# Pairing the modulation products of the closing gates, and scaling block 0's rows at the turn between two layers

## The chip, the core and the metric

The kernel runs on one NeuronCore of a Trainium2 chip. TensorE (PE in the profile) multiplies matrices, VectorE (DVE) and ScalarE (ACT) work element by element, GpSimd (POOL) takes a few small steps, and SyncE (SP) issues the transfers from and to the chip's large memory. Each engine works through its own queue in order; semaphores tie the queues together. The metric is the time of one execution on the device in microseconds (us), the median of several runs; lower is better.

## What is computed

The kernel is one step of a two-layer trunk over 128 context tokens and 256 latent tokens of width 1024. In each layer a vector per request (`c_ctx` for the context, `c` for the latent tokens) is turned into six modulation vectors, and two residual blocks use them:

```python
def trunk_layer(x, cvec, lp, init, latent):
    mod = jax.nn.silu(cvec.astype(jnp.float32)) @ lp['w_mod'] + lp['b_mod']
    sh1, sc1, g1, sh2, sc2, g2 = jnp.split(mod[:, None, :], 6, axis=-1)
    h = rmsnorm(x, lp['norm_mix_pre']) * (1.0 + sc1) + sh1
    mix, states = mixer(h, lp, init, latent)
    x1 = x + g1 * rmsnorm(mix, lp['norm_mix_post'])
    h = rmsnorm(x1, lp['norm_ffn_pre']) * (1.0 + sc2) + sh2
    out = x1 + g2 * rmsnorm(conv_ffn(h, lp), lp['norm_ffn_post'])
    return out.astype(x.dtype), states

def conv_ffn(h, lp):
    up = jnp.einsum('bld,df->blf', h, lp['w_up'])
    a, b = jnp.split(up, 2, axis=-1)
    a = dwconv3(a, lp['ffn_conv_w'], lp['ffn_conv_b'])
    return jnp.einsum('blf,fd->bld', jax.nn.gelu(a, approximate=True) * b, lp['w_down'])
```

The change touches the products that make `g2` (the closing gate of a layer) and the step from the `out` of layer 0 to the `h` of layer 1.

## The kernel before

**Tiling.** The 384 tokens are three blocks of 128, t = 0 (context), 1 and 2 (latent). All large products are made three times with operands split into a high and a low part (`hi`, `lo` of a weight; `hh`, `hl` and `gh`, `gl` of the activations): high by high, high by low, low by high. Each weight tile arrives by a transfer (`raw`); ACT rounds it to `hi` (a CAST, L281), and DVE makes `lo` = raw - hi (L258).

**The feed-forward part** (`ffn`) runs over 32 column pairs p. `up(p)` makes the two halves a and b of pair p: 24 matmuls into PSUM bank 6 and 24 into bank 7, for every p the same two banks. `gated(p)` follows: the convolution `cv` (one ACT instruction and four DVE SCALAR_TENSOR_TENSOR, all of which read bank 6), a GELU on ACT, the product `ge` with bank 7 on DVE, the cast `gh` on ACT and the rest `gl` on DVE. `down(c)` takes the pairs 2c and 2c+1 to the three blocks in 36 matmuls into banks 0 to 5. The loop over c = 0 to 13 does `up(2c+2)`, `up(2c+3)`, `down(c)`.

**The modulation vectors.** Those that are needed later are made beside this loop, by DVE: a queue of generators (`mod_beside`) holds set 3 of the running layer (the closing gate `g2`) and, in layer 0, sets 0 to 2 of layer 1. `beside()` and `fill()` (four in each turn of the loop, after `up(2c+2)`, after `up(2c+3)`, after the first and after the second block of `down(c)`) each let the generator run to its next `yield`. For step i a transfer of one megabyte brings weight rows (`mraw`, two buffers); for each of the two vectors r DVE multiplies four strips of 512 columns by a column of `sil` and adds them to the sum `macc` (L269; the first strip of a sum is written by a TENSOR_SCALAR, L263). Set 3 has four steps i, sets 0 and 1 eight. There is a `yield` after each r, so one call makes four products. After the last one `pe_next` makes `beside()` do nothing until a `fill()`.

**The order.** A scheduler places the instructions on the queues; `issue_after` ties the products of a call behind the DVE instruction written before them, and `high_priority` draws others ahead.

**The turn to layer 1.** After `down(14)` and `down(15)` of a block, `residual` adds it to `x`, and `norm_pre` makes the sum of squares (two ACT Squares), the factor r (POOL), and here a diagonal matrix `diag` of r (DVE, 128x128). Later `norm_P` multiplies the eight pieces of the block's `x` by `diag` on PE, which scales and transposes at once. PE does this for block 0 between `down` of block 1 and of block 2. In the kernel's opening (`start`) the other form is used: `rows=True` scales the rows (`xs`, ACT), and `norm_P` then transposes them.

Of the kernel before, what the change touches and what calls it, by code (L numbers as in the profile page):

```python
# [10 lines left out]
F32 = mybir.dt.float32  # L11
F32R = mybir.dt.float32r
BF16 = mybir.dt.bfloat16
AF = mybir.ActivationFunctionType
ALU = mybir.AluOpType
# [177 lines left out]
class Trunk:  # L193
# [15 lines left out]
    def mm(self, out, lhsT, rhs, start=True, stop=True, **kw):  # L209
        with self.in_order("pe"):  # L210
            self.pe = self.nc.tensor.matmul(out, lhsT=lhsT, rhs=rhs, start=start, stop=stop, **kw)  # L211
# [207 lines left out]
    def start(self, fp):  # L419
# [67 lines left out]
        times(2)  # L487
        times(3)
        for t in range(NT):
            self.norm_pre(t, rows=True)  # L490
        self.use(md=(5,), sm=(6, 7, 0), mm=(0, 1, 2))
        taps = self.filter_taps(fp, 1, hid[1], w3[1])
        times(4)
# [130 lines left out]
    def mod_beside(self, l, s):  # L624

        nc = self.nc
        acc = [self.act_p.tile([128, 2048], F32, tag=t, name=self.nm("macc")) for t in ("hh", "hl")]
        n = KD if s < 2 else KD // 2
        for i in range(n):
            blocks = self.mod_rows(l, s, i)  # L630
            for r in range(2):
                with self.tc.issue_after(self.dve.ins):
                    for k, _, j, raw in blocks:
                        q = slice(512 * j, 512 * j + 512)
                        c = self.sil[:, k, r:r + 1]
                        if k == 0:
                            self.ts(acc[r][:, q], raw, c, ALU.mult)
                        else:
                            self.stt(acc[r][:, q], raw, c, acc[r][:, q], ALU.mult, ALU.add)
                self.pe_next = i == n - 1 and r == 1  # L640
                yield False
        self.pe_next = False
        ps = self.bank(6)

        self.narrow([
            (ps[32 * j:32 * j + 32, :], self.onesel[:, r, :], acc[r][:, 512 * j:512 * j + 512], r == 1, r == 0)
            for r in (1, 0) for j in (3, 0, 1, 2)] if s < 2 else [
            (ps[64 * r + 32 * j:64 * r + 32 * j + 32, :], self.onesel[:, r, :], acc[r][:, 512 * j:512 * j + 512], True, True)
            for r in (1, 0) for j in (1, 0)])
        self.mod_finish(l, s, ps, lambda: self.bank(7), odd=s > 1)  # L650
# [135 lines left out]
        t = lambda n: pool.tile([128, KD, T], F32R, tag=n, name=self.nm(n))  # L786
        return t("hh"), t("hl")

    def norm_pre(self, t, rows=False):

        s2 = self.tiny.tile([128, 2], F32, tag="s2", name=self.nm("s2"), bufs=6)
        for c in range(2):
            jk = self.tmp.tile([128, 512], BF16, tag="junkn", name=self.nm("junk"), bufs=1)
            self.act(jk, self.x[t][:, 512 * c:512 * c + 512], AF.Square, scale=D ** -0.5, accum_out=s2[:, c:c + 1])
        r = self.rms(s2)
        self.scaled[t] = rows
        if rows:
            self.xn[t] = [self.tmp.tile([128, 512], F32, tag="xs", name=self.nm("xs"), bufs=6) for _ in range(2)]
            for c, o in enumerate(self.xn[t]):
                self.act(o, self.x[t][:, 512 * c:512 * c + 512], AF.Copy, scale=r)  # L800
            return
        d = self.tmp.tile([128, 128], F32, tag="diag", name=self.nm("diag"), bufs=3)
        self.ts(d, self.ident, r, ALU.mult)
        self.xn[t] = d
# [659 lines left out]
    def ffn(self, l):  # L1464
        nc = self.nc
        with self.tc.tile_pool(name=f"ffn{l}", bufs=2, reuse_waits="tile") as fp:
# [63 lines left out]
            def down(c, ts=range(NT)):  # L1530
                if c not in ws:
                    ws[c] = self.weights("d", l, c)
                for t in ts:
                    tok = slice(128 * t, 128 * t + 128)
                    blocks = [(gs[p][0][:, tok], gs[p][1][:, tok], w) for p, w in zip((2 * c, 2 * c + 1), ws[c])]
                    self.token_major(accs[t], blocks, c == 0, c == 15)
# [20 lines left out]
            for t in range(NT):  # L1557
                if t == 2 and l + 1 < DEPTH:
                    self.norm_T_after(0, (l + 1, 0, 1, 0, 0), self.h1, lambda c: self.bank(6 + c))
                down(14, [t])  # L1560
                down(15, [t])
                with self.tc.high_priority(offset=300):
                    queues = [nc.sync, nc.scalar, nc.sync] if (l, t) == (DEPTH - 1, NT - 1) else [nc.sync] * 2
                    pieces = ((0, 512), (512, 1024)) if len(queues) == 2 else ((0, 512), (512, 768), (768, 1024))
                    self.residual(t, accs[t], g, pieces, lambda cols: self.store_x(l, t, cols, queues.pop(0)))
                    if l + 1 < DEPTH:
                        self.norm_pre(t)

    def store_x(self, l, t, cols, queue):
        if l + 1 < DEPTH:  # L1570
# [83 lines left out]
```

## Time and profile before

| | us |
|---|---|
| median of 3 runs | 1328.77 (1326.57 to 1328.78) |
| the profiled execution | 1326.61, its span 1324.8 |
| PE busy | 1311.8 |
| DVE busy | 911.2 |
| ACT busy | 571.8 |

The profile is of one execution. Busy times are those of each engine; a matmul on PE is shown longer than the distance to the next one, since they are pipelined, so the distance of two starts is what one costs. Times in rows count from the start of the span.

### The profile page before, as it was taken

The numbers are of one execution on the slowest core, as the hardware profiler recorded it, in microseconds if no ns is written. First come the engines' busy times: TensorE is split into PE (matmuls) and PEld (weight loads), VectorE is DVE, ScalarE is ACT, GpSimd is POOL, SyncE is SP. The second block draws the span as 40 slices with busy tenths as digits, with TensorE's granted clock in tenths as the row PEclk, the third lists the DMA queues.
The fourth block names the chain that finished last, engine by engine and source line by source line (L and its number), as shares of the span: only waits on it lengthen the run. The fifth ranks groups of instructions, "written<-read, shape, count | busy, mean of one in ns | idle before, by whom it ended". The sixth has DMA issues, their size and how long they took to land.

```text
span 1324.8 us, 19348 instructions
## 1 busy us (share of the span) xinstructions
PE 1311.8 (99%) x7465; PEld 1195.3 (90%) x7465; DVE 911.2 (69%) x1635; ACT 571.8 (43%) x950; POOL 34.0 (3%) x64
## 2 busy tenths in 40 slices
PE   8999999999999999999999999999999999999998
PEld 2689999899989989988999999988999999999997
DVE  5748776578879989888476678657885445445445
ACT  4644353473333333333367544446433333333333
POOL 1100000010000000000000000001000000000000
PEclk9999999999999999999999999999999999999999
DMA  9885442625566666665535322442454333333331
GB/s 354 306 311 171 168 137 92 221 79 172 197 218 209 218 208 212 214 215 177 173 122 180 97 84 88 133 148 113 163 182 160 127 126 129 128 127 128 127 124 52
DMA packets 61581, 218.32 MB, mean 165 GB/s; under 512 B 7262, under 2 KB 9760, under 8 KB 58160
## 3 DMA queue, kind: packets, MB, share of 16 engines
q1 hardware_dynamic: 61344, 216.94, 48.0%
q8 instruction: 59, 0.97, 0.3%
q14 instruction: 34, 0.28, 0.1%
q10 hardware_dynamic: 144, 0.13, 0.0%
HBM read 211.11 MB, written 5.94 MB: 164 GB/s over the span
## 4 chain that ended last, share of the span: by engine, by line
PE 93%; DMA 3%; DVE 2%; ACT 1%; issue 1%; POOL 0%; SPq 0%; POOLq 0%; DVEq 0%; ACTq 0%
PE b L211 91%; PE b L215 2%; DMA mraw<-in_w_mod 1%; DMA w<-in_f_w 1%; DMA lo<-in_w_mod 1%; DVE lo L258 1%; DVE x L269 0%; DVE macc L269 0%; POOL rr L294 0%; ACT hi L281 0%; SPq L545 0%; ACT junk L277 0%; DVE macc L263 0%; ACT hf L277 0%; DVE yg L258 0%
## 5 line engine op out<-in xcount | busy, mean ns | idle before, releaser
L258 DVE TENSOR_TENSOR lo<-raw,hi 128x1024 fp32r<-128x1024 f32 (+3 forms) x288 | 320.8, 1128 | 187.0 <-ACT hi L281 184.0
L281 ACT CAST hi<-raw 128x1024 fp32r<-128x1024 f32 (+3 forms) x288 | 275.4, 975 | 385.0 <-PE b L211 376.3
L211 PE MATMUL b<-hh,lo 128*128 128x384 f32 (+1 forms) x1120 | 366.8, 335 | 0.0
L211 PE MATMUL b<-hh,hi 128*128 128x384 f32 (+2 forms) x1120 | 364.0, 334 | 0.0
L211 PE MATMUL b<-hl,hi 128*128 128x384 f32 x1088 | 361.3, 337 | 0.0
L211 PEld LDWEIGHTS b<-hh,hi 128*128 128x128 f32 x1120 | 205.8, 188 | 3.0 <-ACT th L277 0.8
L211 PEld LDWEIGHTS b<-hh,lo 128*128 128x128 f32 x1120 | 208.4, 188 | 0.0
L211 PEld LDWEIGHTS b<-hl,hi 128*128 128x128 f32 x1088 | 203.7, 188 | 1.3
L269 DVE SCALAR_TENSOR_TENSOR cv<-b,pcol,cv 128x127 f32<-128x127 f32 (+1 forms) x256 | 100.5, 414 | 83.3 <-ACT cv L277 79.0
L211 PE MATMUL b<-hi,hh 128*128 128x384 f32 (+2 forms) x444 | 156.1, 355 | 0.0
L211 PE MATMUL b<-lo,hh 128*128 128x384 f32 (+2 forms) x450 | 154.1, 348 | 0.0
L211 PE MATMUL b<-hi,hl 128*128 128x384 f32 (+2 forms) x444 | 153.7, 349 | 0.0
L211 PE MATMUL b<-lo,gh 128*128 128x512 f32 x384 | 151.0, 393 | 0.5 <-DVE lo L258 0.5
L211 PE MATMUL b<-hi,gl 128*128 128x512 f32 x384 | 150.8, 393 | 0.0
L211 PE MATMUL b<-hi,gh 128*128 128x512 f32 x384 | 150.4, 392 | 0.0
L269 DVE SCALAR_TENSOR_TENSOR macc<-mraw,sil,macc 128x512 f32<-128x512 f32 x196 | 132.3, 744 | 0.0
L277 ACT ACTIVATE cv<-b,pcol 128x384 f32<-128x384 f32 x64 | 43.0, 672 | 172.4 <-PE b L211 172.1
L211 PEld LDWEIGHTS b<-hi,gh 128*128 128x128 f32 x384 | 72.1, 188 | 18.7 <-issue 4.2
L211 PEld LDWEIGHTS b<-hi,hl 128*128 128x128 f32 x444 | 83.4, 188 | 5.5 <-issue 1.9
L211 PEld LDWEIGHTS b<-hi,hh 128*128 128x128 f32 x444 | 83.4, 188 | 5.3 <-issue 1.3
L211 PEld LDWEIGHTS b<-lo,hh 128*128 128x128 f32 x450 | 84.6, 188 | 3.3 <-issue 0.5
L211 PEld LDWEIGHTS b<-lo,gh 128*128 128x128 f32 x384 | 72.1, 188 | 15.5 <-DVE lo L258 0.9
(253 smaller groups left out, 1240.4 us busy)
## 6 DMA issues: line engine op xcount, KB each, us to landing
raw<-in_w_up SPq DMA_DIRECT2D x128, 512.0 KB, 4.6
mraw<-in_w_mod SPq DMA_DIRECT2D x40, 1024.0 KB, 8.5
raw<-in_w_down SPq DMA_DIRECT2D x64, 512.0 KB, 4.1
raw<-in_w_in_r SPq DMA_DIRECT2D x32, 384.0 KB, 3.5
raw<-in_w_in_m SPq DMA_DIRECT2D x24, 384.0 KB, 4.6
raw<-in_w_out SPq DMA_DIRECT2D x16, 512.0 KB, 4.5
raw<-in_w_in_h SPq DMA_DIRECT2D x12, 512.0 KB, 4.8
mraw<-in_w_mod SPq DMA_DIRECT2D x8, 512.0 KB, 6.8
```

Of the source, the lines that this page charges most:

```text
L211: self.pe = self.nc.tensor.matmul(out, lhsT=lhsT, rhs=rhs, start=start, stop=stop, **kw)
L215: self.pe = self.nc.tensor.transpose(out, in_, self.ident[:n, :n])
L258: self.dve = self.nc.vector.tensor_tensor(o, a, b, op)
L269: self.dve = self.nc.vector.scalar_tensor_tensor(o, a, s, b, op0, op1)
L277: self.scalar = self.nc.scalar.activation(o, a, f, **kw)
L281: self.scalar = self.nc.scalar.copy(o, a)
```

## The change

It does two things.

First, in `mod_beside` the `yield` after r = 0 is left out for set 3. One call then makes the products of both vectors of a step, eight instead of four, and set 3 takes four calls instead of eight; the sets after it come four calls earlier.

Second, at the turn to layer 1 `norm_pre` of block 0 is called with `rows="both"`: DVE scales columns 0 to 511 of the rows and ACT columns 512 to 1023 (`xs`), no `diag` is made, and `norm_P` transposes `xs` with the identity. Blocks 1 and 2 stay as they were, and so does the opening.

```diff
@@ mod_beside
                 self.pe_next = i == n - 1 and r == 1
-                yield False
+                if r or s < 3:
+                    yield False
         self.pe_next = False
@@ norm_pre
-    def norm_pre(self, t, rows=False):
+    def norm_pre(self, t, rows=None):
...
         if rows:
-            self.xn[t] = [self.tmp.tile([128, 512], F32, tag="xs", name=self.nm("xs"), bufs=6) for _ in range(2)]
+            self.xn[t] = [self.tmp.tile([128, 512], F32, tag="xs", name=self.nm("xs"), bufs=6 if rows == "scalar" else 2) for _ in range(2)]
             for c, o in enumerate(self.xn[t]):
-                self.act(o, self.x[t][:, 512 * c:512 * c + 512], AF.Copy, scale=r)
+                cols = self.x[t][:, 512 * c:512 * c + 512]
+                if rows == "scalar" or c:
+                    self.act(o, cols, AF.Copy, scale=r)
+                else:
+                    self.ts(o, cols, r, ALU.mult)
             return
@@ ffn
                     if l + 1 < DEPTH:
-                        self.norm_pre(t)
+                        self.norm_pre(t, rows="both" if t == 0 else None)
```

The queue of DVE in the first turns of the loop of layer 0, from the `gl` of pair 3 to the convolution of pair 4 (`b_686` is bank 6 of pair 4). Before:

```order
L258 TENSOR_TENSOR lo_3297<-raw_3292,hi_3296 128x1024
L258 TENSOR_TENSOR gl_3283<-ge_3279,gh_3282 128x384
L263 TENSOR_SCALAR macc_3204<-mraw_3205,sil 128x512 x2
L269 SCALAR_TENSOR_TENSOR macc_3204<-mraw_3205,sil,macc_3204 128x512 x2
L269 SCALAR_TENSOR_TENSOR macc_3203<-mraw_3314,sil,macc_3203 128x512 x4
L269 SCALAR_TENSOR_TENSOR macc_3204<-mraw_3314,sil,macc_3204 128x512 x4
L258 TENSOR_TENSOR lo_3355<-raw_3350,hi_3354 128x1024
L258 TENSOR_TENSOR lo_3357<-raw_3352,hi_3356 128x1024
L269 SCALAR_TENSOR_TENSOR cv_3410<-b_686_3348,pcol_166,cv_3410 128x127 x2
L269 SCALAR_TENSOR_TENSOR cv_3410<-b_686_3348,pcol_166,cv_3410 128x255 x2
```

The same stretch with the change (bank 6 of pair 4 is `b_688` here, the weights of pair 5 are `lo_3375` and `lo_3377`, those of `down(1)` are `lo_3450` and `lo_3452`):

```order
L269 SCALAR_TENSOR_TENSOR macc_3203<-mraw_3290,sil,macc_3203 128x512 x4
L269 SCALAR_TENSOR_TENSOR macc_3204<-mraw_3290,sil,macc_3204 128x512 x4
L269 SCALAR_TENSOR_TENSOR macc_3203<-mraw_3324,sil,macc_3203 128x512 x4
L269 SCALAR_TENSOR_TENSOR macc_3204<-mraw_3324,sil,macc_3204 128x512 x4
L269 SCALAR_TENSOR_TENSOR macc_3203<-mraw_3346,sil,macc_3203 128x512 x4
L269 SCALAR_TENSOR_TENSOR macc_3204<-mraw_3346,sil,macc_3204 128x512 x4
L258 TENSOR_TENSOR lo_3375<-raw_3370,hi_3374 128x1024
L258 TENSOR_TENSOR lo_3377<-raw_3372,hi_3376 128x1024
L269 SCALAR_TENSOR_TENSOR cv_3430<-b_688_3368,pcol_166,cv_3430 128x127
L258 TENSOR_TENSOR lo_3450<-raw_3445,hi_3449 128x1024
L269 SCALAR_TENSOR_TENSOR cv_3430<-b_688_3368,pcol_166,cv_3430 128x127
L269 SCALAR_TENSOR_TENSOR cv_3430<-b_688_3368,pcol_166,cv_3430 128x255
```

Twelve products stood between that `gl` and the weights of pair 5; now 24 stand there (the products of step 0 for the second vector have gone ahead, to the call before), and two `lo` of the next weight have moved in between the four instructions of the convolution. The same difference stands in layer 1.

The queue of PE between pair 4 and pair 5. Before, the last matmuls of pair 4 (`b_687`, bank 7) are followed by those of pair 5 (`b_699`, bank 6):

```order
L211 MATMUL b_687_3349<-hl_2598,hi_3296 128x384
L211 MATMUL b_687_3349<-hh_2597,lo_3297 128x384
L211 MATMUL b_699_3429<-hh_2597,hi_3354 128x384
L211 MATMUL b_699_3429<-hl_2598,hi_3354 128x384
L211 MATMUL b_699_3429<-hh_2597,lo_3355 128x384
```

With the change, after the last matmul of pair 4 (pair 5 is `b_700`):

```order
L211 MATMUL b_646_3122<-hi_3449,gh_3199 128x512
L211 MATMUL b_647_3123<-hi_3449,gh_3199 128x512
L211 MATMUL b_648_3124<-hi_3449,gh_3199 128x512
L211 MATMUL b_649_3125<-hi_3449,gh_3199 128x512
L211 MATMUL b_650_3126<-hi_3449,gh_3199 128x512
L211 MATMUL b_651_3127<-hi_3449,gh_3199 128x512
L211 MATMUL b_646_3122<-lo_3450,gh_3199 128x512
L211 MATMUL b_646_3122<-hi_3449,gl_3200 128x512
L211 MATMUL b_646_3122<-hi_3451,gh_3286 128x512
L211 MATMUL b_647_3123<-lo_3450,gh_3199 128x512
L211 MATMUL b_646_3122<-lo_3452,gh_3286 128x512
L211 MATMUL b_700_3443<-hh_2597,hi_3374 128x384
```

Eleven of the 36 matmuls of `down(1)` have moved ahead of `up(5)`; the other 25 stay behind it.

The queue of ACT at the turn (`x_2611` is block 0, `b_648` and `b_649` the sums of block 1). Before:

```order
L277 ACTIVATE junk_6446,s_1161_6445<-x_2611 128x512
L277 ACTIVATE junk_6448,s_1161_6445<-x_2611 128x512
L277 ACTIVATE junk_6482,s_1167_6480<-b_648_3124 128x512
L277 ACTIVATE junk_6485,s_1167_6480<-b_649_3125 128x512
L277 ACTIVATE hf_6512<-b_1179_6507,modT_4647 128x128 x4
L277 ACTIVATE junk_6497,s_1173_6496<-x_2613 128x512
```

With the change:

```order
L277 ACTIVATE junk_6446,s_1161_6445<-x_2611 128x512
L277 ACTIVATE junk_6448,s_1161_6445<-x_2611 128x512
L277 ACTIVATE xs_6455<-x_2611,rr_6452 128x512
L277 ACTIVATE junk_6484,s_1168_6482<-b_648_3124 128x512
L277 ACTIVATE junk_6487,s_1168_6482<-b_649_3125 128x512
L277 ACTIVATE hf_6514<-b_1180_6509,modT_4449 128x128 x4
```

The scaling of block 0 (`xs`) has come ahead of the two Squares of block 1. On PE nothing else moved there.

## Rows read from the trace of the kernel before

**Rows 1.** The page, parts 1 and 4: busy time; the chain that ended last.

```profile
PE 1311.8 (99%) x7465; PEld 1195.3 (90%) x7465; DVE 911.2 (69%) x1635; ACT 571.8 (43%) x950; POOL 34.0 (3%) x64
...
PE 93%; DMA 3%; DVE 2%; ACT 1%; issue 1%; POOL 0%; SPq 0%; POOLq 0%; DVEq 0%; ACTq 0%
```

**Rows 2.** Timeline of DVE, layer 0: start, us, engine, line, operation, [idle before].

```profile
310.58 1.41 DVE L269 SCALAR_TENSOR_TENSOR macc<-mraw,sil,macc 128x512 f32<-128x512 f32 x2
312.22 1.64 DVE L269 SCALAR_TENSOR_TENSOR cv<-b,pcol,cv 128x127 f32<-128x127 f32 x4 [0.22 <-ACT cv L277]
...
317.79 0.55 DVE L258 TENSOR_TENSOR gl<-ge,gh 128x384 fp32r<-128x384 f32 x1
318.26 0.87 DVE L263 TENSOR_SCALAR macc<-mraw,sil 128x512 f32<-128x512 f32 x2
319.06 6.71 DVE L269 SCALAR_TENSOR_TENSOR macc<-mraw,sil,macc 128x512 f32<-128x512 f32 x10
325.69 2.35 DVE L258 TENSOR_TENSOR lo<-raw,hi 128x1024 fp32r<-128x1024 f32 x2
328.94 1.64 DVE L269 SCALAR_TENSOR_TENSOR cv<-b,pcol,cv 128x127 f32<-128x127 f32 x4 [0.91 <-ACT cv L277]
```

**Rows 3.** Timeline of ACT in the same stretch.

```profile
315.57 1.05 ACT L281 CAST hi<-raw 128x1024 fp32r<-128x1024 f32 x1 [0.64 <-PE b L211]
...
323.31 2.00 ACT L281 CAST hi<-raw 128x1024 fp32r<-128x1024 f32 x2 [6.28 <-PE b L211]
328.24 0.67 ACT L277 ACTIVATE cv<-b,pcol 128x384 f32<-128x384 f32 x1 [2.93 <-PE b L211]
```

**Rows 4.** Timeline of PE: first matmul of pair 4, first of pair 5.

```profile
323.80 0.34 PE L211 MATMUL b<-hh,hi 128*128 128x384 f32 x1
...
332.28 0.34 PE L211 MATMUL b<-hh,hi 128*128 128x384 f32 x1
```

**Rows 5.** Timeline of SyncE's issues in the same stretch.

```profile
320.49 5.68 SPq L587 DMA_DIRECT2D mraw<-in_w_mod  x2
```

**Rows 6.** Windows: stretch, us, busy per engine, PEclk, DMA share, GB/s.

```profile
324.00:325.00 1.00, 1.00 (x7) 1.00 (x6) 1.00 (x2) 1.00 (x2) 0.00 (x0) 1.00 0.85 348
325.00:326.00 1.00, 1.00 (x8) 1.00 (x7) 1.00 (x3) 0.30 (x1) 0.00 (x0) 1.00 0.24 98
```

**Rows 7.** The page, part 6: transfers, KB each, median us to landing.

```profile
mraw<-in_w_mod SPq DMA_DIRECT2D x40, 1024.0 KB, 8.5
```

**Rows 8.** Timeline of DVE, the same place in layer 1.

```profile
955.00 6.71 DVE L269 SCALAR_TENSOR_TENSOR macc<-mraw,sil,macc 128x512 f32<-128x512 f32 x10
```

**Rows 9.** Timeline of PE in the kernel's opening.

```profile
8.26 1.41 PE L211 MATMUL b<-fh,w 128*128 128x384 f32 x2 [2.05 <-DMA w<-in_f_w]
```

**Rows 10.** Windows in the opening; the third column from the right is PEclk.

```profile
6.00:9.00 3.00, 0.95 (x3) 0.30 (x2) 1.31 (x3) 0.52 (x1) 0.00 (x0) 0.91 0.97 359
9.00:12.00 3.00, 3.00 (x11) 0.30 (x9) 1.60 (x3) 0.56 (x2) 0.00 (x0) 0.52 1.00 377
```

**Rows 11.** Timeline of DVE at the turn: diagonals of blocks 0 and 1.

```profile
684.77 0.28 DVE L263 TENSOR_SCALAR diag<-c_ident,rr 128x128 f32<-128x128 f32 x1 [0.73 <-POOL rr L294]
...
690.85 0.29 DVE L263 TENSOR_SCALAR diag<-c_ident,rr 128x128 f32<-128x128 f32 x1 [0.41 <-POOL rr L294]
```

**Rows 12.** Timeline of PE at the turn: block 0, first `down` of block 2, block 1.

```profile
685.27 1.95 PE L211 MATMUL b<-diag,x 128*128 128x128 f32 x16
686.97 0.48 PE L211 MATMUL b<-hi,gh 128*128 128x512 f32 x1
...
692.56 1.95 PE L211 MATMUL b<-diag,x 128*128 128x128 f32 x16
```

**Rows 13.** The tile `xs` in the opening: duration in ns, min/median/max.

```profile
L277 ACT ACTIVATE xs<-x,rr x6: 708/720/727, 30.5 to 34.3; 128x512 f32<-128x512 f32 x6
```

**Rows 14.** The chain that ended last, in the opening: eight transposes.

```profile
43.62 1.09 PE b L215 x8
```

More of the change, by code (lines that the diff above doesn't have):

```diff
@@ L489, in start @@
         for t in range(NT):
-            self.norm_pre(t, rows=True)
+            self.norm_pre(t, rows="scalar")
         self.use(md=(5,), sm=(6, 7, 0), mm=(0, 1, 2))
```

## The prediction

> **What bounds the kernel now.** I read the page first: PE is busy 1311.8 of 1324.8 us and 93% of the chain that ended last lies on it, DVE is busy 911.2 us [rows 1]. So a change elsewhere is worth what it takes off PE's queue, or what it makes PE wait. The 69% of DVE is an average. I then read DVE's timeline at the two places that the change touches, in the first turns of the feed-forward loop of each layer and at the turn to layer 1, and beside it ACT, PE and SyncE. In the first place there is to be seen that DVE works almost without a break from 310.58 to the convolution of pair 4 at 328.94 [rows 2]: two stretches of products, with the convolution of pair 3 and the weights between them. PE starts pair 4 at 323.80 and pair 5 at 332.28, with nothing between [rows 4]. Both pairs use bank 6, so pair 5 may start only when the four DVE instructions of pair 4's convolution have read it. They end at 328.94 + 1.64 = 330.58 [rows 2], 1.7 us before PE wants the bank. That is all the room DVE has there.
>
> **Part 1, the paired products: what moves.** No product is added or removed. But the queue of DVE, in the order shown with the change, has 24 products in a row between the `gl` of pair 3 and the weights of pair 5, where 12 stood, and four products of step 0 now stand ahead of pair 3's convolution. DVE takes its queue in order, so behind them wait the `lo` of pair 5, pair 4's convolution and the `lo` of `down(1)`, and behind the convolution waits PE. I follow the queue in the times of the profile.
>
> Step 0, first vector, ends as before at 310.58 + 1.41 = 312.0 [rows 2]. The second vector's four follow: the two TENSOR_SCALAR take 319.06 - 318.26 = 0.80, the others (325.69 - 319.06)/10 = 0.66 each [rows 2], together 2.1, to 314.1. Pair 3's convolution, which started at 312.22, starts there. Its instructions take 1.64 and the two `lo` now among them some 1.15 each, half of 2.35 [rows 2]. The second `lo` needs a cast that ACT ends at 315.57 + 1.05 = 316.6, when a weight buffer comes free [rows 3], so it runs to 317.8; `ge`, ACT's cast and `gl` take about 0.55 each (the `gl` row, rows 2) and end near 319.5. Before, `gl` ended at 318.34. PE does `down(0)` meanwhile, which does not use pair 3: no cost so far, the cover is the 36 matmuls up to 323.80 [rows 4].
>
> Then 24 products at 0.66: 15.9 us, if nothing waits. The weight rows of the last step take the buffer of step 1, so SyncE can issue that megabyte only when eight of the 24 are done, at 324.8. A megabyte that had the queues nearly to itself was issued at 320.49 [rows 5], ran at 348 GB/s in 324 to 325, and by 325 to 326 the rate had fallen to 98 [rows 6]: landed after some 5.6 us. So the last eight can begin at 330.4 instead of 330.1, and end near 335.9. The median of such transfers, most with others beside them, is 8.5 us [rows 7], which would add 2.9; I take 5.6 because the two weight transfers ahead of it have their buffers by 317.8 and nothing else is issued then.
>
> After the burst come the two `lo` of pair 5, 2.35, to 338.2 (their casts on ACT end at 325.3, rows 3), then the convolution of pair 4 with the two `lo` of `down(1)` in it: 1.64 + 2.3, to about 342.1. Before, it ended at 330.58.
>
> PE ends pair 4 at 332.28 as before. The eleven matmuls of `down(1)` that now stand there are worth 11 x 0.23 = 2.5 us (24 of this form from 686.97 to 692.56, rows 12). The first six can run at once, the others need the `lo` made at about 339.7 and 341.5; all fit ahead of 342.1. Since they only come earlier than they did, pair 5 would have started at 332.28 + 2.5 = 334.8 without a wait, and starts at 342.1. **PE loses 7.3 us.** Behind it nothing is late: the `lo` of pair 5 are done at 338.2, bank 7 is free by 343, the products of the next set start only after the small matmuls that close set 3, and everything after that is the old order, one turn of the loop earlier.
>
> Layer 1 has the same queue and the same durations (955.00 and 6.71 for ten products, rows 8), and its order is changed alike: another 7.3 us. Bounds for each layer: 6.5 if the megabyte is in time and the small steps are a little shorter, 10.2 with the 8.5 us landing. A gain is excluded here: PE has no idle time at this place to give back [rows 4].
>
> **The clock after the wait.** PE does nothing from about 333.7 to 339.7 in each layer. In the opening PE waited 2.05 us up to 8.26 [rows 9], and the granted clock was 0.91 over 6 to 9 and 0.52 over 9 to 12 [rows 10]: half of full speed, 1.2 GHz, for 0.54 + 2.88 = 3.4 us in all, though PE had work again. If each of the two waits brings as long a stretch at half, each costs half of it, 1.7 us. Bounds are nothing and, with a second such stretch, 3.4 us. I take 1.7, since these idle times are longer than that in the opening. The Trainium skill says the same of TensorE (TensorE: Matmul & The Clock Gate, Part 1): the clock falls to half after an idle stretch, and sustained activity releases it. By that rule the wait costs more than its own length, and this speaks against the change; without the rule and the row the sum would be 3.4 us less.
>
> **Part 2, the turn.** Before, DVE made the diagonal of block 0 in 684.77 to 685.05 [rows 11], just in time for PE at 685.27, and the 16 records of the product held PE for 686.97 - 685.27 = 1.70 us [rows 12]. Now DVE scales 512 columns in one TENSOR_SCALAR; none of that size from `x` is shown, so I take that of the products, 0.44 to 0.48 each (0.87 for two, rows 2), ending near 685.25. ACT scales the other half in 0.72 [rows 13], from about 684.8 to 685.5, while PE transposes the first. Eight transposes took 1.09 us in the opening with their tail [rows 14], a distance of 0.11, so PE is through near 686.2: 0.8 us gained. Against this stands ACT's queue: its 0.72 comes ahead of block 1's Squares, so block 1's diagonal, ready at 690.85 + 0.29 = 691.1 [rows 11], comes near 691.8, and PE now wants it at 692.56 - 0.8 = 691.8 [rows 12]. The slack is just used up. Later the chain of DVE and ACT, not PE, sets when block 1's columns are ready. I take a gain of 0.5 us, between a gain of 0.8 and a loss of 0.7 (ACT's step paid in full, nothing gained).
>
> **Sum.** 2 x (7.3 + 1.7) - 0.5 = +17.5 us. Made against the profiled execution's 1326.61 this is 1344.1. The median of the runs, 1328.77, lies 2.2 above that execution, so I put the median after half of that higher, at 1345.
>
> **Rivals.**
> - *The wait without the clock.* PE's clock stays up, for the six matmuls and the five others inside the wait speak for activity; against it stands the opening. 1326.61 + 14.6 - 0.5 = 1340.7.
> - *The late megabyte.* The last step's rows land after 8.5 us in both layers: 1326.61 + 2 x (10.2 + 1.7) - 0.5 = 1349.9. For it speaks the median, against it that nothing else is issued.
> - *Not slower: the burst is covered.* If DVE ended pair 4's convolution by 334.8, the eleven matmuls would hide all of it and only the turn would be left, 1326.1. For this the 24 products must take 8.6 us instead of 15.9, at 0.36 each. At the TENSOR_SCALAR's distance of 0.40 they would come near; but ten and ten of the right form show 0.66 in both layers [rows 2, 8].
> - That the change does not do what it says is excluded by the order: the products do stand in a row, and the transposes are there.
>
> **How the numbers follow.** Forecast, wait and clock: 0.62. Wait without the clock 0.18, late megabyte 0.11, covered burst 0.07; 0.02 is left for faster, by nothing that I see in the rows. The range reaches from the lowest waits without the clock, 1326.61 + 13.0 - 0.8 = 1338.8, to the late megabyte on the higher median, 1328.77 + 23.3 = 1352.1: 1338 to 1352. What can be told from no change in this kernel is about 0.2%, 2.7 us. Slower by more has the first three cases, 0.91; within it the covered burst, 0.07; faster 0.02.
>
> **What would show it.** In the changed profile DVE should show 24 products in one row of some 16 us near 319.5 and again some 645 us later, pair 5's first matmul near 342 instead of 332.28, PE idle for 6 us or so before it, and a granted clock below 1 just after. At the turn PE should show eight transposes in about 1 us. The forecast is wrong if pair 5 starts by 335, if the products go faster in a row than one by one, if the clock holds, or if the wait is longer than 10 us because the last megabyte is late.

## The result

The changed kernel took 1343.96 us (median of four, 1342.85 to 1347.24) where the kernel before took 1328.25 in the same series: a ratio of 1.0128, with a 95% interval of 1.0116 to 1.0141. The profile is of the execution of 1347.24 us, whose span is 1345.5.

In the page's first part, PE, DVE and ACT:

```profile
PE 1320.2 (98%) x7457; PEld 1200.1 (89%) x7457; DVE 911.0 (68%) x1635; ACT 572.3 (43%) x951; POOL 33.7 (3%) x64
```

Beside [rows 1] the span has grown by 20.7 us. DVE does what it did, 911 us. PE is busy 8.4 us longer, though eight transposes have taken the place of sixteen records, and idle 25.3 us instead of 13.0 (span less busy). What it waited for stands in the list of PE's waits (who waits <- for whom: us in total, times, longest), of the kernel before:

```profile
PE b L211 <- DVE lo L258: 0.5, 1, 0.5
```

and of the changed kernel:

```profile
PE b L211 <- DVE lo L258: 12.5, 5, 5.3
```

So 12.0 of the 12.3 us of new idle time end at a `lo` that DVE made late: two waits of 5.3 us, one in each layer, and three short ones, two of which stand at the turn.

**Pair 5, layer 0.** DVE's timeline, to be read beside [rows 2]; this execution is 0.69 us later there than the one before, from the opening on:

```profile
313.40 1.41 DVE L269 SCALAR_TENSOR_TENSOR macc<-mraw,sil,macc 128x512 f32<-128x512 f32 x2
...
319.62 0.56 DVE L258 TENSOR_TENSOR gl<-ge,gh 128x384 fp32r<-128x384 f32 x1 [0.58 <-ACT gh L1529]
320.10 16.00 DVE L269 SCALAR_TENSOR_TENSOR macc<-mraw,sil,macc 128x512 f32<-128x512 f32 x24
336.02 2.36 DVE L258 TENSOR_TENSOR lo<-raw,hi 128x1024 fp32r<-128x1024 f32 x2
...
341.46 0.48 DVE L269 SCALAR_TENSOR_TENSOR cv<-b,pcol,cv 128x255 f32<-128x255 f32 x1
```

The 24 products are one row of 16.00 us without a break, 0.67 each, so the last megabyte came in time. The convolution of pair 4 reads bank 6 until 341.94. PE in the same stretch, beside [rows 4]:

```profile
332.97 1.54 PE L211 MATMUL b<-hi,gh 128*128 128x512 f32 x6
339.82 0.80 PE L211 MATMUL b<-lo,gh 128*128 128x512 f32 x1 [5.30 <-DVE lo L258]
...
341.26 1.13 PE L211 MATMUL b<-lo,gh 128*128 128x512 f32 x2
342.20 0.52 PE L211 MATMUL b<-hh,hi 128*128 128x384 f32 x1
```

Pair 5 starts at 342.20, a quarter of a microsecond after bank 6 is free; [rows 4] have 332.28. Without the 0.69 of the opening and the 2.5 us of matmuls that were moved ahead of it, PE has lost 6.7 us. The row at 339.82 names a `lo` of `down(1)` as what ended the idle time. That matmul is one of the eleven that were drawn ahead; pair 5 itself had to wait for bank 6, whose last reader stood behind the same row of products. The last 0.2 us are not DVE's: the eleventh matmul starts at 341.69, and at the half clock of this stretch (below) these stand 0.43 us apart, so PE is through with it at about 342.1, just after the bank is free.

Windows of the same stretch (busy per engine; the third column from the right is the granted clock):

```profile
333.00:336.00 3.00, 1.52 (x7) 0.91 (x5) 3.00 (x5) 1.05 (x1) 0.00 (x0) 1.00 0.18 68
336.00:339.00 3.00, 0.00 (x0) 0.00 (x0) 3.00 (x5) 0.00 (x0) 0.00 (x0) 0.67 0.59 177
339.00:342.00 3.00, 2.18 (x5) 1.46 (x6) 2.94 (x5) 0.00 (x0) 0.00 (x0) 0.50 0.92 321
342.00:345.00 3.00, 3.00 (x13) 3.00 (x13) 1.11 (x2) 1.03 (x2) 0.00 (x0) 0.69 1.02 404
```

The clock fell to its lower level (1.2 GHz) inside the wait and came back 1.7 us into pair 5: 2.0 + 3.0 + 1.9 = 6.8 us at half, by the three windows' clocks, most of it while PE waited or worked on the few matmuls that were moved ahead. The first 48 matmuls of pair 5 took 9.09 us instead of 8.48. In layer 1 pair 5 starts 17.68 us after pair 4 (17.71 in layer 0, 8.48 before) and takes 9.54.

**The turn.** PE, beside [rows 12]:

```profile
692.81 1.09 PE L215 MATMUL b<-c_ident,xs 128*128 128x128 f32 x8
693.66 0.48 PE L211 MATMUL b<-hi,gh 128*128 128x512 f32 x1
...
704.35 0.89 PE L211 MATMUL b<-lo,hh 128*128 128x400 f32 x4
705.71 0.45 PE L211 MATMUL b<-lo,hh 128*128 128x400 f32 x1 [0.48 <-DVE lo L258]
706.92 0.45 PE L211 MATMUL b<-lo,hh 128*128 128x400 f32 x1 [0.76 <-DVE lo L258]
707.21 0.88 PE L211 MATMUL b<-aside,hh 128*128 128x400 f32 x4
```

The transposes hold PE for 0.85 us where the diagonal's product held it for 1.70. But eleven microseconds later, in layer 1's first group, the six products with `lo` (the low parts of that group's weights) take 2.86 us; the kernel before has them in one row of 1.09, from 697.60 to 698.69:

```profile
697.60 1.25 PE L211 MATMUL b<-lo,hh 128*128 128x400 f32 x6
```

DVE at that place, with the change:

```profile
700.63 0.69 DVE L258 TENSOR_TENSOR yg<-b,G 128x512 f32<-128x512 f32 x1
...
702.11 1.42 DVE L269 SCALAR_TENSOR_TENSOR x<-yg,rr,x 128x512 f32<-128x512 f32 x2
703.44 1.05 DVE L258 TENSOR_TENSOR lo<-raw,hi 128x400 fp32r<-128x400 f32 x2
...
705.09 0.57 DVE L258 TENSOR_TENSOR lo<-raw,hi 128x400 fp32r<-128x400 f32 x1
...
706.30 0.57 DVE L258 TENSOR_TENSOR lo<-raw,hi 128x400 fp32r<-128x400 f32 x1
```

and before:

```profile
692.62 0.57 DVE L258 TENSOR_TENSOR lo<-raw,hi 128x400 fp32r<-128x400 f32 x1
693.11 0.68 DVE L258 TENSOR_TENSOR yg<-b,G 128x512 f32<-128x512 f32 x1
693.71 0.56 DVE L258 TENSOR_TENSOR lo<-raw,hi 128x400 fp32r<-128x400 f32 x1
...
696.40 1.05 DVE L258 TENSOR_TENSOR lo<-raw,hi 128x400 fp32r<-128x400 f32 x2
```

The scheduler has put these four `lo` behind the residual of block 2 (`yg`, `x`), where one of them stood ahead of it before, one in it, and the last two, at 696.40, right behind it. The last `lo` now stands behind block 2's `diag` too, for which DVE was idle 0.44 us. This execution is 7.5 us later at the turn; the last `lo` ends 9.4 us later, at 706.87, and PE comes for the six products 0.8 us earlier. So the turn lost 0.8 us instead of gaining.

### The profile page after: what moved, and what is told of

Its sections match the earlier page's. It is cut to its first block, busy times and chain, and to the rows that moved or that the text cites. A ratio compares the mean times of both kernels' runs of the same rounds, so it can differ in the third digit from the quotient of the medians.

```text
span 1345.5 us, 19326 instructions
## 1 busy us (share of the span) xinstructions
PE 1320.2 (98%) x7457; PEld 1200.1 (89%) x7457; DVE 911.0 (68%) x1635; ACT 572.3 (43%) x951; POOL 33.7 (3%) x64
```

## The experiments

Three stretches of PE's timeline are set side by side for each kernel: from the first matmul of pair 4 to the first of pair 8 in layer 0 and in layer 1, and at the turn from the first product that transposes block 0 to layer 1's first product of 384 columns with a high weight (`b<-hi,hh`). They don't depend on what an execution did elsewhere; within a loop's stretch the two spacings of the last section can make some 0.3 us of difference. Times in us; the ratio is to runs of the kernel before on the same chip.

| kernel | median | before | ratio (95%) | layer 0 | layer 1 | turn |
|---|---|---|---|---|---|---|
| before (first profile) | 1328.77 | | | 51.62 | 51.63 | 24.28 |
| changed | 1343.96 | 1328.25 | 1.0128 (1.0116 to 1.0141) | 58.74 | 59.37 | 25.09 |
| changed, again | 1348.13 | 1327.26 | 1.0145 (1.0114 to 1.0176) | 58.90 | 58.92 | 25.11 |
| part 1 alone | 1344.64 | 1328.02 | 1.0124 (1.0098 to 1.0149) | 58.62 | 58.97 | 24.27 |
| part 2 alone | 1328.52 | 1328.02 | 1.0004 (0.9994 to 1.0013) | 51.62 | 51.63 | 25.08 |
| pairs spread | 1327.56 | 1328.02 | 1.0000 (0.9990 to 1.0011) | 51.63 | 51.63 | 24.30 |
| part 2, `lo` first | 1326.72 | 1328.02 | 0.9991 (0.9982 to 1.0001) | 51.63 | 51.63 | 23.33 |
| the same, again | 1326.64 | 1327.21 | 0.9995 (0.9986 to 1.0004) | 51.63 | 51.63 | 23.36 |
| row of 20 | 1335.96 | 1327.26 | 1.0064 (1.0041 to 1.0088) | 54.50 | 55.94 | 24.27 |
| layer 1 only | 1334.89 | 1327.26 | 1.0053 (1.0033 to 1.0072) | 51.63 | 59.73 | 24.31 |
| wait filled | 1341.56 | 1327.26 | 1.0103 (1.0079 to 1.0128) | 57.17 | 57.09 | 24.25 |

**Part 1 alone.** The edit in `mod_beside` without that in `ffn`:

```diff
-                yield False
+                if r or s < 3:
+                    yield False
```

> Part 1 alone; the turn stays as in the kernel before. Theory A (from the changed kernel's trace): all of the loss is the wait of PE ahead of pair 5, 7.1 us net in layer 0 and 7.6 in layer 1, and the turn lost 0.9. Then this kernel takes 1328.3 + 14.7 = 1343.0 us, about 1 us less than the changed kernel where runs of the same matmul spacing are compared; pair 5 starts about 9.2 us later than before (6.7 of wait behind 2.5 of moved matmuls) in both layers; the stretch from the diagonals of block 0 to the first key matmuls of layer 1 takes the same 24.3 us as before. Theory B (the prediction's own terms): 9.0 per layer, and the turn gained 0.5, so 1328.3 + 18.0 = 1346.3 us, above the changed kernel.

Measured: the loop loses 7.00 us in layer 0 and 7.34 in layer 1, the turn is as before. The ratio, 1.0124, can't be told from the changed kernel's, so the whole of what can be measured in the result is part 1. The median lies between A's 1343.0 and B's 1346.3 and does not decide. The two layers' stretches agree with theory A; B's 9.0 for each layer is excluded by them.

**Part 2 alone.**

```diff
-                        self.norm_pre(t)
+                        self.norm_pre(t, rows="both" if t == 0 else None)
```

> Part 2 alone; the products come as in the kernel before. Theory A: the transposes give PE back 0.85 us, but the lo of the next weights stand behind block 2's yg and x on DVE, and PE loses 1.7 us waiting for them; net +0.85 us, 1329.1 us, with PE idle in two pieces (about 0.5 and 0.8 us, ended by lo) some 11 to 14 us after the transposes. Theory B (the prediction): no such wait, net -0.5 us, 1327.8 us. The two differ by 0.1%, so it is the rows that decide: the stretch from the first transpose to the first key matmuls (hi by hh, 128x384) of layer 1 takes 24.3 us before; A expects 25.1, B 23.8. In neither does pair 5 wait.

Measured: the loop is as before in both layers, and the turn takes 25.08 us, 0.80 more. PE shows the two waits again:

```profile
699.46 0.45 PE L211 MATMUL b<-lo,hh 128*128 128x400 f32 x1 [0.46 <-DVE lo L258]
700.67 0.45 PE L211 MATMUL b<-lo,hh 128*128 128x400 f32 x1 [0.76 <-DVE lo L258]
```

The whole kernel can't be told from the one before; the stretch can, and A's 25.1 stands against B's 23.8.

**Part 2 with the `lo` first.** In `ffn`, ahead of block 2's residual, the next weights are split, and the residual is tied behind their last `lo`:

```diff
+                early = nullcontext()
+                if l + 1 < DEPTH and t == 2:
+                    self.prep()
+                    early = self.tc.issue_after(self.dve.ins)
-                with self.tc.high_priority(offset=300):
+                with early, self.tc.high_priority(offset=300):
```

> Part 2 alone, and the weights of the next group are split ahead of block 2's residual on DVE: their lo stand before its yg and x. Theory A: the wait of PE for lo is gone and the gain of the transposes stays, -0.85 us against the kernel before, unless the yg of block 2, 1.1 to 2.2 us later, makes block 2's diagonal late (PE wants it 0.9 us earlier than before; it was ready 2.6 us ahead): 1327.5 to 1328.3 us, and the stretch from the first transpose to the first key matmuls of layer 1 takes 23.4 us. Theory B: the lo never mattered, and this equals the kernel with part 2 alone.

Measured: 23.33 us, 0.95 less than before and 1.75 less than part 2 alone. DVE has the `lo` in one row ahead of `yg`:

```profile
693.11 2.03 DVE L258 TENSOR_TENSOR lo<-raw,hi 128x400 fp32r<-128x400 f32 x4
695.05 0.69 DVE L258 TENSOR_TENSOR yg<-b,G 128x512 f32<-128x512 f32 x1
```

and PE has its six products in one row, and block 2's diagonal in time:

```profile
696.84 1.25 PE L211 MATMUL b<-lo,hh 128*128 128x400 f32 x6
...
700.84 1.95 PE L211 MATMUL b<-diag,x 128*128 128x128 f32 x16
```

So the order of those four instructions, and nothing in the scaling or the transposes, made part 2 a loss. Since this version had the lowest median of all, it ran once more.

> Part 2 with the lo of the next weights ahead of block 2's residual, once more and in more rounds, to see whether it beats the kernel before. Theory A (the stretch of the turn is 0.95 us shorter, 23.33 instead of 24.28, and nothing else differs): the ratio to the kernel before is 0.9993, 1327.3 us beside 1328.2, near the limit of what can be told. Rival: the first series' 0.9991 was chance, and the ratio is 1.000.

The ratio is 0.9995, and its interval holds 1.0000 as well as the expected 0.9993. That the turn is shorter is shown, 23.36 us; that the kernel is faster than the one before is not.

**The pairs spread out.** The products of the closing gate stay paired, but after each pair the generator yields once more, so that every other call makes none:

```diff
+                if s == 3 and r and i < n - 1:
+                    yield False
```

> Part 1 with one edit: after each pair of a step the generator of set 3 yields once more, so that a call that makes eight products is followed by one that makes none. The products are paired, their number is the same, but only eight, not 24, stand between the gl of pair 3 and the weights of pair 5; the turn stays as before. Theory A (the row of 24 in front of the convolution of pair 4 is what costs): no wait at pair 5 in either layer, half clock nowhere in the loop, 1328.3 us within 1.5. Rival C (the pairing itself costs, by the eight products in one piece ahead of a convolution or by the buffers of the weight rows): waits of some us remain, 1332 us or more.

Measured: no loss anywhere. DVE in layer 0, the stretch of [rows 2]:

```profile
318.93 0.75 DVE L269 SCALAR_TENSOR_TENSOR macc<-mraw,sil,macc 128x512 f32<-128x512 f32 x1
319.60 0.56 DVE L258 TENSOR_TENSOR gl<-ge,gh 128x384 fp32r<-128x384 f32 x1
320.07 4.72 DVE L269 SCALAR_TENSOR_TENSOR macc<-mraw,sil,macc 128x512 f32<-128x512 f32 x7
325.07 2.36 DVE L258 TENSOR_TENSOR lo<-raw,hi 128x1024 fp32r<-128x1024 f32 x2 [0.27 <-ACT hi L281]
329.62 1.64 DVE L269 SCALAR_TENSOR_TENSOR cv<-b,pcol,cv 128x127 f32<-128x127 f32 x4 [2.19 <-ACT cv L277]
```

Eight products stand there, one ahead of `gl` and seven behind it, and DVE is idle for 2.19 us ahead of pair 4's convolution, where [rows 2] had 0.91. Pairing costs nothing; what costs is that three pairs came in a row.

**A row of 20.** The last four products of set 3 are left out:

```diff
-                    for k, _, j, raw in blocks:
+                    for k, _, j, raw in (() if s == 3 and i == n - 1 and r == 1 else blocks):
```

> Part 1 alone, leaving out the last four products of each closing gate (the second vector of the last step), so that 20 stand in the row instead of 24; the closing gate of the latent tokens lacks that step. Theory A (PE waits for DVE, which works through the row at 0.66 us a product): the row is 2.65 us shorter, pair 5 starts 2.65 us earlier in each layer apart from the down matmuls that are moved ahead of it, the wait is 4.1 us instead of 6.7, and the whole is 5.3 us shorter than part 1 alone, 1337.7 us at the narrower spacing of the matmuls (up to 3.7 more at the wider). Rival (the wait has another end, such as the last megabyte or the lo of pair 5): the wait stays at 6 us or more, 1342 us or above.

Measured: 4.1 us less than part 1 alone in layer 0 and 3.0 in layer 1, 7.1 in all, where A expected 5.3 and its rival nothing. Against pair 4, DVE is through with bank 6 2.5 us earlier than in part 1 alone (337.99 instead of 341.46 in layer 0, where pair 4 starts at 323.04 and 324.01), near A's 2.65. But the scheduler now puts 17 matmuls of `down(1)` ahead of pair 5 instead of 11, and in layer 0 pair 5 starts only behind them, 2.2 us earlier than in part 1 alone. With the 1.4 us of the six more, and the 0.6 of half clock that pair 5 no longer pays, that is the 4.1. With all 17 counted the wait is 3.1 us in layer 0 and 4.5 in layer 1. The layers differ by the clock. PE in layer 0 and in layer 1:

```profile
335.86 0.50 PE L211 MATMUL b<-lo,gh 128*128 128x512 f32 x1 [2.80 <-DVE lo L258]
...
338.50 0.34 PE L211 MATMUL b<-hh,hi 128*128 128x384 f32 x1
...
976.07 0.79 PE L211 MATMUL b<-lo,gh 128*128 128x512 f32 x1 [2.74 <-DVE lo L258]
...
980.17 0.34 PE L211 MATMUL b<-hh,hi 128*128 128x384 f32 x1
```

and the windows behind the two waits:

```profile
336.00:339.00 3.00, 3.00 (x14) 2.53 (x15) 2.35 (x5) 0.53 (x1) 0.00 (x0) 1.00 0.91 313
...
975.00:978.00 3.00, 1.93 (x5) 1.54 (x6) 3.00 (x5) 0.00 (x0) 0.00 (x0) 0.64 0.97 302
978.00:981.00 3.00, 3.00 (x13) 2.54 (x12) 1.30 (x3) 1.04 (x2) 0.00 (x0) 0.79 0.77 285
```

After an idle time of 2.80 us the clock held, and after one of 2.74 it fell, in the same execution. In layer 1 the moved matmuls then stand 0.43 us apart instead of 0.23: DVE is through with bank 6 at 978.19, and pair 5 starts 2.0 us later (0.5 in layer 0).

**Layer 1 only.**

```diff
-                yield False
+                if r or s < 3 or l == 0:
+                    yield False
```

> Pairing in layer 1 only; layer 0 and the turn as before. Theory A: layer 0 shows no wait at pair 5, layer 1 shows the 6.7 us and costs 7.6 in all: 1335.7 us, or up to 1339.4 if the matmuls of layer 1 keep the wider spacing. Rival (the loss of one layer is partly paid back or doubled by the other): another sum than half of part 1 alone.

Measured: layer 0 as before, layer 1 loses 8.10 us. Pair 5 starts 17.69 us after pair 4, as in all the others, but its first 48 matmuls take 10.21 us, since the half clock here began later in the wait and lasted longer into the work:

```profile
979.00:982.00 3.00, 3.00 (x11) 3.00 (x10) 1.11 (x2) 0.76 (x2) 0.00 (x0) 0.50 0.83 291
982.00:985.00 3.00, 3.00 (x16) 3.00 (x16) 0.00 (x0) 0.00 (x0) 0.00 (x0) 0.88 0.13 52
```

The layers add up: neither pays back or doubles what the other loses.

**The wait filled.** Part 1 alone, and behind pair 4 another 24 matmuls of zeros, which add nothing to the sums (the lines that make the tile of zeros are left out here):

```diff
+                if c == 1:
+                    for _ in range(24):
+                        with self.tc.high_priority(offset=300), self.tc.issue_after(self.pe.ins):
+                            self.mm(accs[0][0][:64].rearrange("p (a n) -> p a n", a=8), self.zero[:, 0], self.zero.to_broadcast([128, 8, 64]), False, False)
```

> Part 1 alone, with 24 matmuls more behind pair 4 in the second turn of the loop of each layer, whose operands are zeros and which add nothing to the sums (64 rows, 512 columns): they fill most of the 5.3 us in which PE does nothing. Theory A with the clock term: PE's granted clock stays at 1.00 through the wait, the first 48 matmuls of pair 5 take 8.3 to 8.5 us instead of 9.1 to 9.5, and the whole is 1 to 2 us shorter than part 1 alone at the same spacing, though PE has more work. Rival (the half clock has nothing to do with the idle PE): the granted clock falls as before and pair 5 takes 9.1 or more. If the added matmuls outlast the wait, pair 5 starts later and the whole is longer; the rows of pair 5 then decide alone.

Measured: with more work PE loses 1.5 us less in layer 0 and 1.9 less in layer 1. PE and the windows in layer 0:

```profile
332.85 5.37 PE L211 MATMUL b<-zero 128*64 128x512 bf16 x24
...
342.37 0.34 PE L211 MATMUL b<-hh,hi 128*128 128x384 f32 x1
```

```profile
337.00:339.00 2.00, 2.00 (x10) 1.13 (x9) 2.00 (x4) 0.00 (x0) 0.00 (x0) 1.00 1.00 283
339.00:341.00 2.00, 2.00 (x9) 1.38 (x8) 2.00 (x4) 0.00 (x0) 0.00 (x0) 1.00 0.98 365
```

The clock stays at 1.00, and pair 5's first 48 matmuls take 8.48 and 8.38 us. So it is the idle PE that brings the half clock here, and beside part 1 alone (9.09 and 9.47) 0.6 and 1.1 us of the gain are the clock's. The rest is the order's: here too 17 matmuls of `down(1)` stand ahead of pair 5, six more than in part 1 alone, worth 1.4 us, against 0.3 to 0.4 by which pair 5 starts later.

**The changed kernel again.**

> The changed kernel once more, unchanged. In the first profile of it the up matmuls (128x384) of layer 1 stand 0.1766 us apart to the end, where the kernel before and part 1 alone show 0.1734 for most of the layer; 12 turns of 96 matmuls make 3.7 us of that. Theory: the distance is not set by the kernel's code but by the execution, so the runs of this kernel fall in two groups, near 1343.5 and near 1347.2 us, and a second profile may show 0.1734 where the first had 0.1766. Rival: the distance belongs to this program, every run has it, and the runs lie in one group. Either way the waits at pair 5 are 6.7 us in both layers and the stretch at the turn takes 25.1 us.

Measured: 1341.91 to 1350.41 us, the profiled execution 1347.33. The waits and the turn are those of the first profile. The runs do not fall into two clear groups, so the theory's first half is not borne out; its second half is, in part (last section).

## Why the prediction was right

The forecast of 1345 lies 1.0 us above the first series' median (and 3.1 below that of the second), and its mechanism for part 1 is the one that the runs show. But not every term had its size, the turn had the wrong sign, and that the time came so near is partly luck: the terms as measured come to 15.3 us instead of 17.5, the kernel before took 0.8 us more than the 1327.5 that the forecast started from, and the spacing of the last section moves an execution by as much as 3.7.

- **The row of 24 and the bank.** Shown, by the trace and by the pairs spread out. Moved by the 0.69 us of the opening, the forecast's times were 314.8 for the end of the four products of step 0, 320.2 for `gl` and 342.8 for the convolution's end; measured were 314.7, 320.1 and 341.9. The megabyte was there in time, which the forecast had cost at 0.3, and the `lo` and convolutions overlapped a little more than their rows' lengths said. The wait is 6.7 us in each layer that has the row of 24 and no added matmuls, against 7.3 forecast, inside the bounds; PE's idle time in it is 5.3 us, against 6.0.
- **The clock.** The mechanism is shown by the filled wait. The size, 1.7 for each layer, was the mis-sized term of part 1: pair 5 lost 0.55 to 1.06 us in three profiles with both layers paired and 1.73 in the one with layer 1 alone. The step that failed is "If each of the two waits brings as long a stretch at half, each costs half of it": the stretch was twice the opening's, 6.8 us, but most of it lay in the wait, where it made pair 5 only some 0.2 us later (an estimate, from the matmul at 341.69 above). In these profiles what is paid is what is left of it when pair 5 begins.
- **A rule on the clock.** The Trainium skill (TensorE: Matmul & The Clock Gate, Part 1) says that an idle engine falls to the half clock, and that how many matmuls run slow varies between runs. All waits with 5.3 us of idle time agree with the first, and the 0.55 to 1.73 us above with the second; after 2.8 us the clock fell in one layer and held in the other.
- **The sum of part 1.** 7.0 to 7.3 in layer 0 and 7.3 to 7.7 in layer 1 (8.1 where layer 1 stands alone), against 9.0 each: 3 to 4 us too much in all. They are a little less than 6.7 plus what pair 5 lost, where the turn behind has the narrower spacing.
- **The turn.** Wrong in sign: 0.8 us lost instead of 0.5 gained. The transposes gave the 0.85 forecast as 0.8, and block 1's diagonal came just in time, at 698.85 to 699.14 for PE's 699.25. What failed is the step "Later the chain of DVE and ACT, not PE, sets when block 1's columns are ready. I take a gain of 0.5 us": it followed block 1's diagonal and not the `lo` of layer 1's first weights, which had moved on the same queue. The measured 0.8 lies outside its bounds by 0.1.
- **What made up for it.** The terms as measured, 7.1 + 7.4 + 0.8 = 15.3, stand beside the 15.7 between the medians of the first series. The first profiled execution is longer, by 20.7 in the span: 7.1 + 7.7 + 0.8 for these terms, 0.7 in the opening, 0.8 between the turn and layer 1's loop (most of it a wait for `q`), and 3.7 for the wider spacing below.
- **The rivals.** The late megabyte and the covered burst did not come about. The covered burst had not been followed through to the end either: with products of 0.36 the last megabyte, issued at 322.4 and 5.6 us on its way, would by the prediction's own times have held the last eight products until 328.0 and the convolution until about 337, later than the 334.8 that it needs. The wait without the clock was nearer in its price (14.1 us, beside the 15.3 measured and the forecast's 17.5), but its reason is wrong: the clock did fall.

## What to carry over

An engine that is 69% busy may have no room where it counts: count what stands in its queue ahead of the instruction that frees a buffer, and spread optional work so that no call puts more there than the slack (1.7 us here, against 12 more products of 0.66). When a scheduler re-orders a queue, follow every instruction that moved to whoever waits for it, small ones too; four `lo` of half a microsecond each, put in another place, undid the gain of a better transpose. A stall of TensorE can cost more than its length: here, behind 5.3 us of idle time, whatever part of the 6.8 us at half clock outlasted it, 0.55 to 1.73 us.

## What was not expected of the hardware

The up matmuls (128x384, all of one form) stand in most turns either 0.1766 or 0.1734 us apart, at a granted clock of 1.00, and keep one or the other for a turn of the loop or many; in single turns the mean is 0.1746. Here are the first matmul of pairs 16 and 17 and the first after their 96, in the first profile of the changed kernel,

```profile
485.33 0.34 PE L211 MATMUL b<-hh,hi 128*128 128x384 f32 x1
...
501.97 0.39 PE L211 MATMUL b<-hi,gh 128*128 128x512 f32 x1
```

and in the second:

```profile
484.98 0.34 PE L211 MATMUL b<-hh,hi 128*128 128x384 f32 x1
...
501.94 0.39 PE L211 MATMUL b<-hi,gh 128*128 128x512 f32 x1
```

16.64 and 16.96 us for the same 96 matmuls of the same kernel: here the execution sets it, not the code. The code has a part all the same: in layer 1 all five profiles without the wait show the same order, wide to pair 7, 0.1746 in pairs 8 and 9, narrow from there on. In layer 1 both profiles of the changed kernel and that of the filled wait show the wide spacing from pair 6 to the end, 0.32 us for each turn of 96; part 1 alone, the row of 20 and layer 1 only show the narrow one from pair 8 at the latest. Most changes fall at the turns with the narrow matmuls that close a modulation set, or at the wait. What decides which spacing follows stays open, and so does how much of the runs' spread (1341.9 to 1350.4 for the changed kernel) it makes. Part 1 alone, whose profile of 1342.40 us has the narrow spacing in layer 1, took 1341.36, 1342.40, 1346.89 and 1347.03 us; whether the two longer ones had the wide spacing was not seen.
